# One layer of an S5 / GLA / cross-attention decoder on one core: the S5 factors queued behind the splits of the first projection's weights

## The chip, the core and the metric

The kernel runs on one core of one Trainium2 chip. The metric is the device time of one execution in microseconds (us), the median of the timed runs. The engines are TensorE (PE in the profile, its weight loads PEld), VectorE (DVE), ScalarE (ACT), GpSimd (POOL) and SyncE (SP), which here only issues transfers.

## The reference, cut to what matters

The layer takes 1024 tokens of 1024 numbers. The change touches the beginning of the layer: the input projection and the preparation of the S5 head group.

```
z = h @ w_in                              # h = layer_norm(x); columns u | q k | v | r | gate rank
y_ssm = s5_mixer(z[..., :512], lam, log_step, b, c, d, w_glu, b_glu)
y_gla = gla_mixer(q, k, v, r, g_lr, ...)
...
step = exp(log_step); a = exp(lam * step)            # 32 groups x 64 complex states
f = (a - 1) / lam                                    # f_re, f_im: num * conj(lam) / |lam|^2
bb = f * b                                           # complex, (group, state, 16)
bu = einsum(u, bb); s = associative_scan(a, bu); y = Re(c s) + d u
...
h = LN(alpha h + concat(y_ssm, y_gla) @ w_out); h = LN(alpha h + cross_attention(h, mem)); h = LN(alpha h + mlp(h))
```

## The kernel before, in words

**Products in split float32.** Every large product is made of three products of rounded halves. `split` (L150) makes the halves of a tile: ScalarE writes the rounded high half (`hi`), and then VectorE or GpSimd writes the rest (`lo = src - hi`). `mm3` (L160) issues hi x hi, hi x lo and lo x hi for each 128-wide slice. So a weight tile can be used by the first product of a slice when its `hi` is there, and must have its `lo` by the third. Weights arrive 256 rows at a time (`wcols`, L203): a transfer into a `raw` buffer, of which there are four, and a split into a `w` buffer, of which there are five. Which engine makes the `lo` is chosen by a bit mask; for the u weights the mask `MWU` is 7: pieces 0, 1 and 2 on VectorE, piece 3 on GpSimd.

**The beginning of the layer.** Some work on the memory tokens comes first. Then eight tiles of 128 tokens are normalised and transposed (`embed`), interleaved with the r columns of the projection (`z_block` with `wr`), with `r_epi` behind each. Then come the small gate projection (L529 to L535), the last r block (L536) and the split of the four u weight pieces (`wu`, L537). The last r block and the u weights share buffers: piece 0 of `wu` sits in the fifth buffer and is split early, and pieces 1 to 3 can be split only when the last r block has passed the matching piece of `wr`.

**The S5 factors.** Lines 555 to 716 compute everything that depends only on the S5 parameters, nearly all on VectorE and nearly all on 128 x 16 tiles named `prm` and `par`: exponentials, sine and cosine, the powers `pw`, the rotation tables `E0` and `E1`. Lines 677 to 692 then compute the factor f (`nre`, `den`, `fre`, `fim`). Lines 693 to 698 multiply it with b on GpSimd into `Bb`, and lines 701 to 716 build comparison masks for a later stage.

**Batches of S5.** The 16 pairs of groups go in eight batches of two pairs. A batch passes through the stages `s5_t0` (L749: three outer products on VectorE: C with the powers, `Vt`, 128 x 288 wide; `Bb` with the powers, `wtmp`, 128 x 256 wide; `E0` with `E1`, `rot`, 128 x 256 wide, which runs on GpSimd for all batches but the first, since `CM` is 1), `s5_t1` (transposes), `s5_t2` (taps), `s5_m1` (loads u), `s5_m2` (scan) and `s5_m3` (output). In the traces the tiles of a batch are named `s`; the order rows number them, `s_1341` for the first batch and `s_1360` for the second.

**The u, q, k and v projections.** `z_stream` (L891) yields blocks of 24 products of 128x512. The first two are u columns 0 to 127 for the two halves of the tokens, and so on; behind each of the first four blocks comes a `gate` (L540): one small product, three ScalarE passes, two VectorE operations (`gst`) and a transfer. `Filler.run(n)` runs the stream for n units, where a block yields 5.1. Before the change `fill.run(FP)` with `FP` = 30 runs six blocks, and then the first S5 stages follow.

**What sets the order.** The program is written as one stream. A scheduler places each engine's instructions by its own estimates, as dependences allow, and each engine then executes its list strictly in that order. So the source order around the change is a priority, not the order on the engine. The helper `behind()` (L131) makes the VectorE instructions inside its block queue behind the VectorE instruction traced last.

Of the kernel before, what the change touches and what calls it, by code (L numbers as in the profile page):

```python
# [1 line left out]

# [29 lines left out]
FP = 30  # L32
# [49 lines left out]
def hybrid_layer(  # L82
# [8 lines left out]
    nc = tc.nc  # L91
    V = nc.vector
# [31 lines left out]
    def slot(name, shape, dtype=F32):  # L124
        return arena.tile(shape, dtype, tag="s", name=name)
# [2 lines left out]
        return psp.tile(list(shape), F32, tag=tag, bufs={"d": 3, "s": 3, "g": 2}[tag], name="ps_" + tag)  # L128


    def behind():  # L131

        return tc.issue_after(next(i for i in reversed(nc.cur_bb.bb.instructions) if i.engine == V.engine))

    def ts(e, o, i, s1, s2=None, op0=ALU.mult, op1=None):
        if s2 is None:
# [53 lines left out]
    def eng(bits, i):  # L190
        return V if bits >> i & 1 else G


    def weight(src, shape, e=nc.vector, hl=None):

        raw = rawp.tile(shape, F32, tag="raw", name="raw")
        nc.sync.dma_start(out=raw, in_=src)
        if hl is None:
            hl = wp.tile([P, 2] + list(shape[1:]), F32R, tag="w", name="hl")
        split(hl[:, 0], hl[:, 1], raw, e=e)  # L200
        return hl

    def wcols(src, k0, c0, e=nc.vector, hl=None):  # L203
        return weight(src[k0 * P:(k0 + 2) * P, c0:c0 + 512].rearrange("(k p) n -> p k n", p=P), [P, 2, 512], e, hl)
# [75 lines left out]
    for b in range(4):  # L280
        z = (b + 1) % 3 * 512 + 512
# [47 lines left out]
    def alternate(*streams):  # L329

        streams = [(iter(z), n) for z, n in streams]
        while streams:
            for z in list(streams):
                for _ in range(z[1]):
                    c = next(z[0], None)
                    if c is None:
                        streams.remove(z)
                        break
                    yield c
# [81 lines left out]
    def z_block(w, tok, t, epi):  # L421
        po = bank()
        for k in range(8):
            mm3(po, lambda i: tok(h0(k, i), t), lambda j: w[k // 2][:, j, k % 2, :], k == 0, k == 7)
        epi(t, po)
# [14 lines left out]
    fill = Filler(mem_stream([0], "g", slot("wo0", [P, 2, 2, 2, 512], F32R)))  # L440
# [61 lines left out]
    def pt(n=1):  # L502
        i = scr_n[0]
        scr_n[0] += n
        return scr[:, i, :] if n == 1 else scr[:, i:i + n, :]

    e = V
# [27 lines left out]
        act(glr[th], po[0:32])  # L535
    z_block(wr, tok_block, NT - 1, r_epi)  # L536
    wu = [wcols(w_in, 2 * kp, 0, eng(MWU, kp)) for kp in range(4)]  # L537
    srs.pop()()

    def gate(th, a):  # L540
# [60 lines left out]
    def cmul(e, o_re, o_im, a_re, a_im, b_re, b_im, t):  # L601
        tt(e, o_re, a_re, b_re, ALU.mult)
        tt(e, t, a_im, b_im, ALU.mult)
        tt(e, o_re, o_re, t, ALU.subtract)
        tt(e, o_im, a_re, b_im, ALU.mult)
        tt(e, t, a_im, b_re, ALU.mult)
        tt(e, o_im, o_im, t, ALU.add)
# [56 lines left out]
    for Et, cnt in ((E0, 16), (E1, 8)):  # L664
        G.memset(Et[:, 0, 0, :], 1.0)
        G.memset(Et[:, 1, 0, :], 0.0)
        n = 1
        while n < cnt:
            bc = [z.unsqueeze(1).to_broadcast([P, n, NJ]) for z in (pr, pi_)]
            cmul(e, Et[:, 0, n:2 * n, :], Et[:, 1, n:2 * n, :], Et[:, 0, 0:n, :], Et[:, 1, 0:n, :],  # L670
                 bc[0], bc[1], te[:, 0:n, :])
            o = (pt(), pt())
            cmul(e, o[0], o[1], pr, pi_, pr, pi_, tw[:, 0, :])
            pr, pi_ = o
            n *= 2

    nre, den, fre, fim = (pt() for _ in range(4))
    tt(e, nre, mag1, cs, ALU.mult)
# [189 lines left out]
    def s5(stage_, i):  # L868
        if i < NBT:
            if stage_ is s5_t0:  # L870
                bat[i] = Batch(i)
            stage_(bat[i])

    for i in range(2):
        s5(s5_t0, i)


    qk = slot("qk", [P, 4, SEQ])
# [12 lines left out]
    def z_stream():  # L891

        wqk = []
        for fo in range(4):
            us = stage.tile([P, T, P], F32, tag="kv", bufs=1, name="us")
            for th in range(2):
                po = z_fm(wu, fo, th)
                act(us[:, :, th * 64:(th + 1) * 64], po.rearrange("p (c t) -> p t c", t=T))
                if th:
                    nc.scalar.dma_start(out=u_d[fo * P:(fo + 1) * P], in_=us)  # L900
                if gates:
                    gate(*gates.pop(0))
                if fo == 3:
                    wqk += [wcols(w_in, 2 * kp, 512, eng(MQK, kp)) for kp in (2 * th, 2 * th + 1)]
                yield 5.1

        wv = []
        for fo in range(4):
            for th in range(2):
                po = z_fm(wqk, fo, th)  # L910
                act(qk[:, fo, th * 512:(th + 1) * 512], po, scale=0.125 if fo < 2 else 1.0)
                if fo == 3:
                    wv += [wcols(w_in, 2 * kp, 1024, eng(MVV, kp)) for kp in (2 * th, 2 * th + 1)]
                yield 5.1

        for t in range(NT):
            if t == 1:
                wgl.append(wcols(w_glu, 0, 0))
            po = bank()
            for k in range(8):  # L920
                mm3(po, lambda i: tok_block(h0(k, i), t), lambda j: wv[k // 2][:, j, k % 2, :], k == 0, k == 7)
            vs = stage.tile([P, 512], F32, tag="rt", bufs=3, name="vs")
            act(vs, po)
            nc.scalar.dma_start(out=v_d[t * P:(t + 1) * P, :], in_=vs)
            yield 5.1

    mem_rest = mem_stream([1, 2, 3], "d")
    fill = Filler(z_stream(), mem_rest)
    fill.run(FP)
    s5(s5_m1, 0)  # L930
    s5(s5_t1, 0)
    s5(s5_t2, 0)
# [63 lines left out]
    def y_split(th, k):  # L996
        hi, lo = (ya(0, th)[:, i, k, :].rearrange("p (c t) -> p c t", t=T) for i in range(2))
        with behind():
            split(hi, lo, Y0[:, k, :].rearrange("p (t c) -> p c t", t=T)[:, th * 64:(th + 1) * 64, :], scale=0.25)
# [11 lines left out]
    def glu_stream():  # L1011

        for k in range(4):
            nc.sync.dma_start(out=Y0[:, k, :], in_=y_d[k * P:(k + 1) * P].rearrange("f t c -> f (t c)"))
        for k in range(4):
            if k == 2:
                wgl.append(wcols(w_glu, 2, 0))
            split(glu_s[0][:, k, :], glu_s[1][:, k, :], Y0[:, k, :])
        yield 0
        for fo in range(4):  # L1020
            for th in range(2):
                cs_ = slice(th * 512, (th + 1) * 512)
                po = bank()
                for k in range(4):
                    mm3(po, lambda i: wgl[k // 2][:, i, k % 2, fo * P:(fo + 1) * P], lambda j: glu_s[j][:, k, cs_],
                        k == 0, k == 3)
                sg = sg_[th]
                act(sg, po, AF.Tanh, scale=0.25, bias=bglu[:, fo:fo + 1])
                stt(V, Y0[:, fo, cs_], sg, 1.0, Y0[:, fo, cs_], ALU.add, ALU.mult)
                yield 2.6  # L1030
        for th in range(2):
            for k in range(4):
                y_split(th, k)
                yield 0.5
        load_res(0)

    def out_stream():

        load_res(1)
        w = []  # L1040
        for n in range(2):
            w += [wcols(w_out, 2 * kp, n * 512, eng(MWS, 2 * n + kp)) for kp in range(2)]
        yield 0
        for n in range(2):
            for t in range(NT):
                po = bank()
                for k in range(4):
                    mm3(po, lambda i: ya.lhs(k, i, t), lambda j: w[2 * n + k // 2][:, j, k % 2, :], k == 0, k == 3)
                r = res(t)[:, n * 512:(n + 1) * 512]
                stt(V, r, r, ALPHA, po, ALU.mult, ALU.add)  # L1050
                yield 2.6

    fill = Filler(alternate((glu_stream(), 1), (fill, 1)), out_stream())
# [342 lines left out]
    for _ in range(2):  # L1396
        z = wp.tile([P, 2, 2, 512], F32R, tag="w", name="w1q")
# [202 lines left out]
    def half_stats(m):  # L1600
        with behind():
            for n in range(2):
                stats(m, n)
            if m == 3:
                first.extend(last_stats(range(4)))

    def norm_half():
        with behind():
            last_norm(*first.pop(0))
# [127 lines left out]
```

## Time and profile before

| | us |
|---|---|
| median of 3 runs | 1384.01 (1383.97 to 1388.86) |
| the profiled execution, its own time | 1385.14 |
| its span | 1383.3 |
| what lies around the span | 1.8 |
| PE busy in the span | 1336.5 (97%) |
| DVE busy | 966.8 (70%) |
| ACT busy | 569.6 (41%) |
| POOL busy | 410.4 (30%) |

A row of the timeline gives the start, the time, the engine, the line, the operation, out<-in, shapes and count; behind it in brackets the idle time before it and what ended it. Consecutive operations on one engine overlap a little, so that the sum of their times is more than the time from the first start to the last end. A line such as L142 or L163 is a helper's: the tile names tell which step it is. A row of waits has the total, the number of times and the longest, in us.

### The profile page before, as it was taken

To read this page: it belongs to the slowest core of one execution; us is meant where nothing else is said; L and a number is where in the kernel's file an instruction comes from. 1 tells how busy PE (TensorE), PEld (TensorE's weight loads), DVE (VectorE), ACT (ScalarE), POOL (GpSimd) and SP (SyncE) were. 2 spreads that over 40 slices of the span, in tenths; PEclk is the share of its full clock that TensorE was granted. 3 is DMA by queue.
4 is the path that set the end of the run, shared out by engine and by line. 5 is a ranking of instruction groups with operands and counts; after the bars stand their busy time and mean duration, and the time that the engine had idled before them with its cause. 6 is when DMAs were issued, how large, how long until landed. Compare 5 with 4: busy or idle time off the path is not lost. (4 is left out here: it accounts for less than half of the span.)

```text
span 1383.3 us, 18805 instructions
## 1 busy us (share of the span) xinstructions
PE 1336.5 (97%) x6824; PEld 1110.4 (80%) x6824; DVE 966.8 (70%) x1713; ACT 569.6 (41%) x950; POOL 410.4 (30%) x315
## 2 busy tenths in 40 slices
PE   6798999999999999999999999999999999999997
PEld 6575777788899888788888778788888888888886
DVE  8999587947965369844468866665565576668785
ACT  4432532323545244433123755455456343344441
POOL 1663133502334133000013124433332242003353
PEclk9999999999999999999999999999999999999999
DMA  9832332454576130310212657654446984235432
GB/s 303 264 122 69 120 104 65 126 171 137 201 258 214 48 92 23 122 31 0 62 46 61 183 167 228 214 167 158 160 139 238 328 309 145 94 110 163 136 107 91
DMA packets 155512, 199.81 MB, mean 144 GB/s; under 512 B 16294, under 2 KB 86044, under 8 KB 155292
## 3 DMA queue, kind: packets, MB, share of 16 engines
q1 hardware_dynamic: 143536, 179.44, 40.0%
q10 hardware_dynamic: 11884, 19.17, 3.7%
q8 instruction: 54, 0.88, 0.3%
q14 instruction: 38, 0.31, 0.1%
HBM read 140.38 MB, written 58.20 MB: 144 GB/s over the span
## 5 line engine op out<-in xcount | busy, mean ns | idle before, releaser
L163 PE MATMUL ps_d<-xt,w1q 128*128 128x512 f32 x576 | 137.2, 389 | 0.0
L163 PEld LDWEIGHTS ps_d<-xt,w1q 128*128 128x128 f32 x576 | 108.1, 188 | 22.4
L163 PE MATMUL ps_s<-cell 128*128 128x512 f32 x432 | 113.0, 389 | 0.0
L163 PE MATMUL ps_d<-cell 128*128 128x512 f32 x432 | 106.0, 389 | 0.4 <-DVE hid L142 0.4
L163 PE MATMUL ps_d<-h0T,hl 128*128 128x512 f32 x384 | 93.1, 400 | 5.8 <-DVE hl L142 5.8
L163 PEld LDWEIGHTS ps_d<-cell 128*128 128x128 f32 x432 | 81.0, 188 | 17.6 <-DVE hid L142 0.8
L163 PEld LDWEIGHTS ps_s<-cell 128*128 128x128 f32 x432 | 81.1, 188 | 16.8
L163 PE MATMUL ps_d<-hl,h0T 128*128 128x512 f32 x384 | 92.5, 398 | 1.3 <-DVE h0T L142 1.3
L148 ACT ACTIVATE hl<-raw 128x1024 fp32r<-128x1024 f32 x62 | 65.3, 1064 | 68.9 <-PE ps_d L163 61.9
L163 PEld LDWEIGHTS ps_d<-h0T,hl 128*128 128x128 f32 x384 | 72.8, 192 | 25.7 <-DVE hl L142 6.2
L163 PE MATMUL ps_d<-hl,y 128*128 128x512 f32 x384 | 92.4, 395 | 0.0
L163 PE MATMUL ps_g<-xb,w1q 128*128 128x512 f32 x384 | 92.1, 391 | 0.0
L163 PE MATMUL ps_d<-hl,p 128*128 128x512 f32 x384 | 89.0, 391 | 0.0
L148 ACT ACTIVATE hid<-hid 128x512 f32<-128x512 f32 x112 | 70.8, 632 | 38.9 <-DVE hid L142 37.1
L163 PEld LDWEIGHTS ps_d<-hl,h0T 128*128 128x128 f32 x384 | 72.2, 191 | 17.4 <-DVE h0T L142 1.8
L142 DVE TENSOR_TENSOR cell<-ha,cell 128x1024 fp32r<-128x1024 f32 x56 | 82.4, 1472 | 3.3 <-ACT cell L148 3.3
L163 PEld LDWEIGHTS ps_d<-hl,p 128*128 128x128 f32 x384 | 71.6, 188 | 14.6
L163 PEld LDWEIGHTS ps_g<-xb,w1q 128*128 128x128 f32 x384 | 71.5, 188 | 14.6
L163 PEld LDWEIGHTS ps_d<-hl,y 128*128 128x128 f32 x384 | 70.7, 188 | 14.6 <-issue 0.3
L142 DVE TENSOR_TENSOR hl<-raw,hl 128x1024 fp32r<-128x1024 f32 x50 | 66.4, 1336 | 21.0 <-ACT hl L148 20.5
L148 ACT ACTIVATE w1q<-raw 128x512 fp32r<-128x512 f32 x80 | 50.1, 629 | 69.3 <-PE ps_d L163 27.3
L142 POOL TENSOR_TENSOR hl<-raw,hl 128x1024 fp32r<-128x1024 f32 x12 | 33.6, 2806 | 142.0 <-ACT hl L148 142.0
(296 smaller groups left out, 2802.8 us busy)
## 6 DMA issues: line engine op xcount, KB each, us to landing
g_d<-hid SPq DMA_DIRECT2D x112, 256.0 KB
ha<-g_d SPq DMA_DIRECT2D x56, 512.0 KB
raw<-in_w_ff_dram SPq DMA_DIRECT2D x40, 512.0 KB
b<-in_w_ff_dram SPq DMA_DIRECT2D x32, 512.0 KB
raw<-in_w_mkv_dram SPq DMA_DIRECT2D x16, 512.0 KB
raw<-in_w_in_dram SPq DMA_DIRECT2D x16, 512.0 KB
wq<-in_w_mq_dram SPq DMA_DIRECT2D x8, 512.0 KB
xs<-in_x_dram SPq DMA_DIRECT2D x8, 512.0 KB
```

The lines of the kernel that those rows point to most:

```text
L142: e.tensor_tensor(out=o, in0=a, in1=b, op=op)
L148: A.activation(out=o, in_=i, func=f, **kw)
L163: PE.matmul(o, lhs(i), rhs(j), start=first and n == 0, stop=last and n == 2, skip_group_check=more)
```

## The change

Three edits. First, `behind` takes the instructions to queue behind as arguments. Second, the VectorE instruction traced last after the u weights are split is kept as `split_u` (it is the `lo` of piece 2), and every VectorE instruction written from the computation of `nre` (L677 before) up to the end of the first batch's `s5_t0` queues behind it. Third, the second batch's `s5_t0` is no longer written next to the first's, but after two blocks of the u projection. Instructions of GpSimd and of ScalarE are not pinned; they follow through their dependences and the scheduler's order.

```diff
-    def behind():
-        return tc.issue_after(next(i for i in reversed(nc.cur_bb.bb.instructions) if i.engine == V.engine))
+    def traced(e):
+        return next(i for i in reversed(nc.cur_bb.bb.instructions) if i.engine == e.engine)
+
+    @contextmanager
+    def behind(*ins):
+        with ExitStack() as z:
+            for i in ins or (traced(V),):
+                z.enter_context(tc.issue_after(i))
+            yield
...
     wu = [wcols(w_in, 2 * kp, 0, eng(MWU, kp)) for kp in range(4)]
+    split_u = traced(V)
...
+    order = ExitStack()
+    order.enter_context(behind(split_u))
+
     nre, den, fre, fim = (pt() for _ in range(4))
...
-    for i in range(2):
-        s5(s5_t0, i)
+    s5(s5_t0, 0)
+    order.close()
...
-    fill.run(FP)
+    fill.run(10)
+    s5(s5_t0, 1)
+    fill.run(FP - 10)
```

On VectorE, around the splits of pieces 1 and 2 of `wu` (`hl<-raw,hl`), the order before the change reads as follows; `prm` and `par` are S5 parameter tiles, `s_1360` is the second batch.

```order
L142 TENSOR_TENSOR s_1360<-par 128x256
L142 TENSOR_TENSOR prm<-par,prm 128x16
L142 TENSOR_TENSOR par<-par,prm 128x16
L142 TENSOR_TENSOR prm<-prm 128x16
L142 TENSOR_TENSOR hl<-raw,hl 128x1024
L142 TENSOR_TENSOR par<-par,prm 128x16
L142 TENSOR_TENSOR prm<-prm 128x16 x2
L142 TENSOR_TENSOR hl<-raw,hl 128x1024
```

After the change (line 142 is line 150 there) the same place, and the beginning of what is pinned; `s_1341` is the first batch.

```order
L150 TENSOR_TENSOR par<-par,prm 128x64
L150 TENSOR_TENSOR prm<-prm 128x16 x2
L150 TENSOR_TENSOR hl<-raw,hl 128x1024 x2
L150 TENSOR_TENSOR prm<-prm 128x16 x4
L150 TENSOR_TENSOR prm<-par,prm 128x16
L150 TENSOR_TENSOR prm<-prm 128x16
L150 TENSOR_TENSOR prm<-par,prm 128x16
L150 TENSOR_TENSOR s_1341<-par 128x288
L695 RECIPROCAL prm<-prm 128x16
```

The two splits now stand next to each other, ahead of every operation on a batch, and behind all of the powers and rotation tables, of which 31 small operations stood behind the first split before.

On GpSimd, before the change, from the end of the six operations of `Bb` (`prm<-prm` and `par<-par,prm` are the last two of them) past the r block's epilogue (`rt`) and the split of piece 3 to the second batch's rotation:

```order
L142 TENSOR_TENSOR prm<-prm 128x256
L831 MEMSET s_1360 128x2
L142 TENSOR_TENSOR par<-par,prm 128x256
L142 TENSOR_TENSOR rt<-rt,prm 128x512
L790 MEMSET s_1341 80x2x128
L879 MEMSET qk 128x1
L1065 MEMSET S 128x256
L142 TENSOR_TENSOR hl<-raw,hl 128x1024
L142 TENSOR_TENSOR s_1360<-par 128x256 x4
L142 TENSOR_TENSOR s_1360<-s_1360 128x256 x2
```

After the change, where the second batch has the name `s_1436`:

```order
L150 TENSOR_TENSOR rt<-rt,prm 128x512
L1079 MEMSET S 128x256
L150 TENSOR_TENSOR hl<-raw,hl 128x1024
L891 MEMSET qk 128x1
L150 TENSOR_TENSOR s_1436<-par 128x256 x4
L150 TENSOR_TENSOR s_1436<-s_1436 128x256 x2
L843 MEMSET s_1436 128x2
L150 TENSOR_TENSOR par<-prm 128x256
L717 IOTA prm 128x128
L150 TENSOR_TENSOR prm<-prm 128x256
```

The six operations of `Bb` have moved from ahead of the split of piece 3 to behind the second batch's rotation, which itself still follows that split.

On VectorE, at the first of the four gates (`gst`), before the change:

```order
L142 TENSOR_TENSOR s_1341<-s_1341 128x256
L137 TENSOR_SCALAR prm<-prm 128x128
L142 TENSOR_TENSOR s_1360<-s_1360 128x256
L145 SCALAR_TENSOR_TENSOR mask<-prm 128x64
L142 TENSOR_TENSOR s_1360<-s_1360 128x256
L137 TENSOR_SCALAR prm<-prm 128x128
L139 TENSOR_SCALAR gst<-ps_s,bgate 128x512
L145 SCALAR_TENSOR_TENSOR mask<-prm 128x64
L142 TENSOR_TENSOR hl<-raw,hl 128x1024
```

After the change:

```order
L145 TENSOR_SCALAR prm<-prm 128x128
L150 TENSOR_TENSOR s_1341<-par 128x256
L153 SCALAR_TENSOR_TENSOR mask<-prm 128x64
L150 TENSOR_TENSOR s_1341<-s_1341 128x256 x2
L147 TENSOR_SCALAR gst<-ps_s,bgate 128x512
L150 TENSOR_TENSOR s_1436<-par 128x288
L150 TENSOR_TENSOR gst<-gst 128x512
L150 TENSOR_TENSOR s_1436<-par 128x288 x3
```

The first gate now stands behind the whole first batch and behind the last mask; the second batch's twelve VectorE operations stand between the first gate's first operation and the second gate's last, where before they were all ahead of the first gate's.

The order on PE is the same in both programs. On ACT one small copy of the second batch moves behind the u weights' high halves. On SP one later weight load moves behind the u loads of the first two batches.

More of the change, by code (lines that the diff above doesn't have):

```diff
@@ L1 @@
-from contextlib import ExitStack
+from contextlib import ExitStack, contextmanager
 import concourse.bass as bass
```

## The prediction

> **What bounds the kernel now.** The page comes first: PE is busy for 97% of the span, so only what makes PE wait, or makes its clock fall, can change the time.
>
> ```profile
> span 1383.3 us, 18805 instructions
> PE 1336.5 (97%) x6824; PEld 1110.4 (80%) x6824; DVE 966.8 (70%) x1713; ACT 569.6 (41%) x950; POOL 410.4 (30%) x315
> ```
>
> The waits of PE in the first 420 us come next. The longest single one is a wait for `hl`, a `lo` of the u weights, which is where the change acts.
>
> ```profile
> PE ps_d L163 <- DVE hl L142: 5.8, 1, 5.8
> ```
>
> The timeline of PE shows where it is and what follows it.
>
> ```profile
> 117.32 1.98 PE L163 MATMUL ps_d<-h0T,hl 128*128 128x512 f32 x8
> 125.08 6.15 PE L163 MATMUL ps_d<-h0T,hl 128*128 128x512 f32 x16 [5.78 <-DVE hl L142]
> 131.15 1.12 PE L543 MATMUL ps_s<-prm 32*128 32x512 f32 x2
> ...
> 138.94 5.73 PE L163 MATMUL ps_d<-h0T,hl 128*128 128x512 f32 x24
> ...
> 151.32 1.12 PE L543 MATMUL ps_s<-prm 32*128 32x512 f32 x2
> ```
>
> Eight products of the first u block run: six on piece 0 and two on piece 1. Then PE stands for 5.78 us until the `lo` of piece 1 exists. The remaining 16 products take 6.15 us, though a block of 24 takes 5.73, which is 0.239 each and 3.82 for 16. The windows of one microsecond say why.
>
> ```profile
> 122.00:123.00 1.00, 0.00 (x0) 1.00 0.00 0
> 123.00:124.00 1.00, 0.00 (x0) 0.52 0.00 0
> 129.00:130.00 1.00, 1.00 (x4) 0.57 0.84 250
> 130.00:131.00 1.00, 1.00 (x6) 1.00 1.03 305
> ```
>
> The granted clock (the column before the last two) falls to half some 4 us into the wait, and is full again only at 130.
>
> Why the split comes late is read from VectorE's timeline and its groups between 95.1 and 123.8 us.
>
> ```profile
> 95.19 0.43 DVE L569 COPY par<-prm 128x512 f32<-128x512 f32 x1 [0.33 <-POOL xs L142]
> ...
> 118.24 2.37 DVE L142 TENSOR_TENSOR prm<-prm 128x16 f32<-128x16 f32 x1
> ...
> 123.81 1.22 DVE L142 TENSOR_TENSOR hl<-raw,hl 128x1024 fp32r<-128x1024 f32 x1
> ```
>
> ```profile
> L142 DVE TENSOR_TENSOR s<-par 128x288 f32<-128x288 f32 x8 | 4.1, 518 | 0.0
> L142 DVE TENSOR_TENSOR s<-par 128x256 f32<-128x256 f32 x6 | 2.5, 419 | 0.0
> ...
> L145 DVE SCALAR_TENSOR_TENSOR rt<-rt,ps_d 128x512 f32<-128x512 f32 x2 | 1.4, 680 | 0.0
> ...
> L142 DVE TENSOR_TENSOR par<-par,prm 128x16 f32<-128x16 f32 x8 | 1.3, 165 | 0.0
> ...
> L142 DVE TENSOR_TENSOR s<-s 128x288 f32<-128x288 f32 x2 | 0.9, 449 | 0.0
> L145 DVE SCALAR_TENSOR_TENSOR s<-s 128x288 f32<-128x288 f32 x2 | 0.9, 448 | 0.0
> L142 DVE TENSOR_TENSOR s<-s 128x256 f32<-128x256 f32 x2 | 0.8, 422 | 0.0
> ```
>
> VectorE has no idle time from 95.19 to 123.81: it works through factors and batches, and the split stands in that list. Its input was there long before, since ScalarE wrote the three high halves from 114.76 on:
>
> ```profile
> 114.76 2.94 ACT L148 ACTIVATE hl<-raw 128x1024 fp32r<-128x1024 f32 x3
> ```
>
> **The change part by part.**
>
> *The splits go ahead of the batches.* Out of the list before the split go 20 batch operations, 4.1 + 2.5 + 0.9 + 0.9 + 0.8 = 9.2 us busy. An operation starts about 0.08 before its forerunner ends, so this is 7.6 us of clock. Into it come 31 small operations on powers and tables that stood behind the first split: at 0.165 each 5.1 us at most, 2.6 with the overlap. The operation at 118.24, 16 elements wide, took 2.37 us. GpSimd's timeline shows why, and what GpSimd does next.
>
> ```profile
> 117.78 2.80 POOL L142 TENSOR_TENSOR hl<-raw,hl 128x1024 fp32r<-128x1024 f32 x1 [3.87 <-ACT hl L148]
> 130.47 4.41 POOL L142 TENSOR_TENSOR s<-par 128x256 f32<-128x256 f32 x4 [9.89 <-DVE prm L142]
> 134.84 1.73 POOL L142 TENSOR_TENSOR s<-s 128x256 f32<-128x256 f32 x2
> ```
>
> It ended at 120.61, when GpSimd's split of piece 3 ended at 120.58. In the new order VectorE should be at the splits before that begins, which takes off another 2.3 us. So VectorE comes to them at 123.81 - 7.6 - 2.3 + 2.6 = 116.5 (latest, without the last two savings, 123.81 - 7.6 + 5.1 = 121.3). I take 116.5, since the operations of `Bb`, which ran beside this stretch, have left it too. The `lo` of piece 1 is then ready at 117.7 and that of piece 2 at 118.9. PE needs them at 117.32 + 1.98 = 119.30 and, six products on, at 120.7. Piece 3, on GpSimd, ends at 120.6 and is needed 20 products in, at 122.1; its place behind ScalarE is not later than before. So the wait goes whole: **-5.78**. With it goes the clock's fall, 6.15 - 3.82: **-2.33**. Late next would be piece 3, with 1.5 us to spare.
>
> From then on PE is 8.1 us ahead: the first gate's product at 123.05 instead of 131.15, the fourth's at 143.2 instead of 151.32.
>
> *What the pinned work delays.* Behind the splits stand some 14 small operations and a reciprocal, the last r block's epilogue, three integer and ten mask operations, and the first batch's 18. The integer and mask operations are priced by this group of the stretch from 124.9 to 143 us:
>
> ```profile
> L137 DVE TENSOR_SCALAR prm<-prm 128x128 f32<-128x128 f32 x5 | 1.1, 221 | 0.1
> ```
>
> The clock of all, with nothing in the way, each row's mean less the overlap of 0.08: 15 x 0.09 + 2 x 0.6 + 13 x 0.14 + 6 x 0.37 + 12 x 0.34, so 10.7 us, which I round up to 11.4 for the integer types, and an end at 118.9 + 11.4 = 130.3. In the way is GpSimd, which now runs the second batch's rotation (4.41 + 1.73 = 6.1 us) directly behind piece 3 and then `Bb`, six operations of the same 256 columns, so 6.1 at most. If VectorE loses all of that it ends at 142.5. Then comes the first gate's `gst`.
>
> ```profile
> 138.58 0.74 DVE L139 TENSOR_SCALAR gst<-ps_s,bgate 128x512 f32<-128x512 f32 x1
> ...
> 140.65 0.68 DVE L142 TENSOR_TENSOR gst<-gst 128x512 f32<-128x512 f32 x1
> ```
>
> It ran at 138.58 and I take 139.5 for it, near the upper end, because `Bb` needs the pinned `fre` and `fim` and the batch needs `Bb`. Who waits for it: the fourth gate's product, as there are three banks of `ps_s`, at 143.2; and ScalarE at the third gate, whose buffer comes free with the first gate's transfer. Until 143.2 it costs PE nothing; at the upper end of 142.5 still nothing, though the third gate then starts late on ScalarE. The gates had cover, which the waits between 120 and 200 us show:
>
> ```profile
> DVE gst L142 <- ACT gst L148: 3.6, 2, 3.1
> ...
> DVE gst L139 <- ACT gst L148: 2.1, 1, 2.1
> ```
>
> VectorE waited 5.7 us for ScalarE within the gates. The second batch's twelve operations, 6 x 0.37 + 6 x 0.34 = 4.3 us, now fill this time instead of preceding it. PE comes to the first batch's transposes here:
>
> ```profile
> 163.39 0.60 PE L783 MATMUL ps_g<-ident,s 128*128 128x128 f32 x4
> ```
>
> That is 155.3 in the new time, over 12 us after the first batch is done, and the second batch's are 4.4 us later, for operations that end near 147. I take **+0.3** for the additions to the taps, which stand behind the last gate in VectorE's list; bounds 0 and +5, if the chain of gates on ScalarE runs late. The order of SP moves one weight load behind u loads; its piece belongs to q and k, behind eight blocks of u, so it costs nothing. The factor's own operations leave the stretch before 95 us, where they are some eight of 0.09: nothing, bounds -1 and +0.5.
>
> Sum: -5.78 - 2.33 + 0.3 = **-7.8**. Against the profiled execution, 1385.14 - 7.8 = 1377.3. That execution lies 1.1 above the median, so on the median's scale 1384.01 - 7.8 = **1376.2**. After 200 us PE's list is the same and PE sets the pace, so the lead should be carried to the end.
>
> **A shorter wait that stays, weighed against the skill.** An earlier wait of PE shows what a rest of 2 to 3 us would cost.
>
> ```profile
> 77.86 0.65 PE L251 MATMUL ps_s<-ident,xs 128*128 128x128 f32 x4 [2.36 <-POOL xs L142]
> 78.27 7.35 PE L163 MATMUL ps_d<-hl,h0T 128*128 128x512 f32 x24
> ```
>
> After only 2.36 us of idleness 24 products took 7.35 instead of 5.73, so 1.6 us more. The Trainium skill ("TensorE: Matmul & The Clock Gate", Part 1) says that the clock is halved after at least one idle window of about 3.4 us; by that a rest under 3.4 us would cost no clock. The row disagrees, and I price by the row.
>
> **The rivals.**
>
> *Part of the wait stays.* If VectorE reaches the splits at 121.3, the `lo` of piece 1 comes at 122.5, PE waits 3.2 us and the clock takes 1.6 more: 7.8 - 4.8, so a gain of 3.0 and 1381.0. For it: small operations stretch next to GpSimd, as at 118.24. Against it: from 117.7, where I put the end of the first split, to 119.3 there are 1.6 us of margin. Chance 0.13.
>
> *The gates come late.* If the first `gst` comes at 145 or its successors each push ScalarE back, PE loses 2 to 5 us at the fourth gate or at the transposes: a gain of about 4, 1380. Chance 0.12.
>
> *The lead is given back.* A later wait, on a transfer or on VectorE in the S5 loop, might absorb it: 1384. PE's later waits are short, which speaks against it. Chance 0.07.
>
> *Slower.* The pinned block, GpSimd's rotation, `Bb` and the first batch become one chain: `Bb` waits for the rotation and for `fim`, the batch waits for `Bb`, the first gate for the batch. The place is VectorE's first `gst`. Each microsecond past 143.2 is one on PE's fourth gate; at 151.3 the lead is gone, and at 158 the time is 1391. For that, the 48 pinned operations would need 39 us, 0.8 us each, three and a half times the 11.4 of their sum. The Trainium skill ("SBUF — State Buffer", Who interferes with whom) says that a VectorE operation with two SBUF inputs and a GpSimd operation that reads SBUF lock each other out for a whole instruction. By that rule alone, which the operation at 118.24 bears out, VectorE loses at most GpSimd's busy time, which is the 142.5 above. Chance 0.08.
>
> **How the numbers follow.** The forecast has 0.60. About 0.5%, or 6.9 us, is what a measurement of this kernel can tell from no change, and it lies at 1377.1, only 0.9 from the forecast. The spread of the forecast is -1.5 to +1.5 (the bounds of the small terms), so I count 0.50 of the 0.60 beyond it and 0.10 short of it. Faster 0.50; same 0.10 + 0.13 + 0.12 + 0.07 = 0.42; slower 0.08. The range runs from 1374.2, two below the forecast, to 1382.5, which takes in the first two rivals.
>
> **What would show it.** Right: no PE wait for `hl` near 119, the clock at 1.00 from 117 to 131, the first gate's product near 123.05, the fourth's near 143.2 without a wait, the first transposes near 155.5. Wrong: a rest of the wait at 119; `gst` on VectorE later than 143 with PE idle before the fourth gate; or a lead of 8 us at 155 that is smaller at 350 or 600.

## The result, and the profile after

| | before | after |
|---|---|---|
| median, us | 1384.17 (8 runs, 1381.14 to 1388.86) | 1376.62 (8 runs, 1373.27 to 1381.32) |
| ratio after/before, 95% interval | | 0.9949 (0.9938 to 0.996) |
| profiled execution, its own time, us | 1385.14 | 1376.45 |
| its span, us | 1383.3 | 1374.4 |

The change takes 7.55 us off the median; the ratio puts the gain at 0.51%, with an interval from 0.4% to 0.62%. The forecast was 1376.2. The page of the changed kernel first:

```profile
span 1374.4 us, 18808 instructions
PE 1333.9 (97%) x6824; PEld 1108.2 (81%) x6824; DVE 968.6 (70%) x1713; ACT 569.6 (41%) x950; POOL 410.6 (30%) x315
```

The busy times are almost those of before; PE's is 2.6 us shorter, of the size of what the half clock behind the old wait had cost (the clock fell at other places too, not at the same ones in both traces). The rest that went is waiting. Of PE's wait for a `lo` of the u weights, this is left among its waits of the first 420 us (total, times, longest):

```profile
PE ps_d L171 <- DVE hl L150: 0.6, 1, 0.6
```

PE's timeline shows the u block at 117.69, with one short stop after 14 products instead of a long one after eight, and then the first gate, the fourth, and the first batch's transposes:

```profile
117.69 3.33 PE L171 MATMUL ps_d<-h0T,hl 128*128 128x512 f32 x14
121.64 2.56 PE L171 MATMUL ps_d<-h0T,hl 128*128 128x512 f32 x10 [0.61 <-DVE hl L150]
124.13 1.12 PE L552 MATMUL ps_s<-prm 32*128 32x512 f32 x2
...
144.27 1.12 PE L552 MATMUL ps_s<-prm 32*128 32x512 f32 x2
145.32 11.18 PE L171 MATMUL ps_d<-h0T,hl 128*128 128x512 f32 x48
156.34 0.60 PE L795 MATMUL ps_g<-ident,s 128*128 128x128 f32 x4
```

Against the rows of before these three are earlier by 131.15 - 124.13 = 7.02, 151.32 - 144.27 = 7.05 and 163.39 - 156.34 = 7.05. In this execution the block itself started 0.37 later (117.69 against 117.32), so the block gained 7.4. None of that was lost from the first gate to the transposes: there is no bracket at the fourth gate. The time by which PE is ahead of the first trace of before, at the same product, is called the lead from here on. The granted clock (the column before the last two), which fell to half in the old wait, stays at full speed around the stop:

```profile
121.00:122.00 1.00, 0.39 (x3) 1.00 0.36 137
122.00:123.00 1.00, 1.00 (x6) 1.00 0.41 23
```

Why a stop is left is seen on VectorE and GpSimd. VectorE's timeline first, with the two splits of pieces 1 and 2 in one row, what follows them, and the first gate:

```profile
117.02 4.56 DVE L150 TENSOR_TENSOR hl<-raw,hl 128x1024 fp32r<-128x1024 f32 x2
121.51 1.60 DVE L150 TENSOR_TENSOR prm<-prm 128x16 f32<-128x16 f32 x4
...
138.47 0.73 DVE L147 TENSOR_SCALAR gst<-ps_s,bgate 128x512 f32<-128x512 f32 x1
139.13 0.43 DVE L150 TENSOR_TENSOR s<-par 128x288 f32<-128x288 f32 x1
139.50 0.67 DVE L150 TENSOR_TENSOR gst<-gst 128x512 f32<-128x512 f32 x1
```

GpSimd's timeline over the same time, piece 3's split and then the second batch's rotation:

```profile
117.67 2.83 POOL L150 TENSOR_TENSOR hl<-raw,hl 128x1024 fp32r<-128x1024 f32 x1 [4.90 <-ACT hl L156]
...
120.51 4.00 POOL L150 TENSOR_TENSOR s<-par 128x256 f32<-128x256 f32 x4
```

The second split's own row shows how the 4.56 us are divided:

```profile
118.16 3.43 DVE L150 TENSOR_TENSOR hl<-raw,hl 128x1024 fp32r<-128x1024 f32 x1
```

The first split took 1.2 us, the second 3.4. It ends at 121.58, 1.08 after GpSimd's split ended at 120.50: the second split moved only when GpSimd was done (e8 below tests this), and PE stood for it from 121.03 to 121.64.

The gates had their cover, the time by which their delayed work may be late without PE waiting for it. VectorE waits for ScalarE within them hardly any more (5.7 us before), and ScalarE's third gate starts late, held by the transfer of the first, with no PE wait behind it:

```profile
DVE gst L150 <- ACT gst L156: 0.2, 1, 0.2
```

```profile
142.71 0.69 ACT L156 ACTIVATE gst<-ps_s,bgate 128x512 f32<-128x512 f32 x1 [4.45 <-DMA gk_d<-gst]
```

The spans of the two profiled executions differ by 8.9 us, 1.8 more than the 7.05 at the transposes. What came on top lies behind 200 us and is not the change's. The trace of before has a wait in the S5 loop that the trace of after lacks, with the clock's fall behind it:

```profile
217.15 0.49 PE L852 MATMUL ps_s<-s 64*128 64x128 f32 x4 [1.60 <-DVE s L142]
```

```profile
219.00:220.00 1.00, 1.00 (x12) 0.50 0.00 0
```

Between 215 and 225 us the lead grows from 7.09 to 9.94, and 1.1 of that is lost again behind 1000 us. e1 and e3 below, which still have the old wait for the split, gain 2.8 and 2.5 in the same place against the first trace of before; so this part was a loss of that one execution. e5 and e6 show too that such waits come and go between executions of one kernel.

### The profile page after: what moved, and what is told of

It is laid out like the page before. It is cut to its first block, busy times and chain, and to the rows that moved or that the text cites. A ratio compares the mean times of both kernels' runs of the same rounds, so it can differ in the third digit from the quotient of the medians.

```text
span 1374.4 us, 18808 instructions
## 1 busy us (share of the span) xinstructions
PE 1333.9 (97%) x6824; PEld 1108.2 (81%) x6824; DVE 968.6 (70%) x1713; ACT 569.6 (41%) x950; POOL 410.6 (30%) x315
```

## The experiments

The theory that the runs were to test: the pin (VectorE's queueing behind `split_u`) brings the splits forward, PE's wait and the half clock behind it vanish, and cover up to 143 us hides what is delayed. The rivals: the place of the second batch does it; the wait alone counts and the clock does not; the gates eat the lead; the lead is lost again in the S5 loop. All ratios below are set against runs of the kernel before on the same chip, so they are not the quotients of the medians in the table. "Block to gate" is the time from the first product of the u block to the first gate's product, which does not depend on when an execution reaches the block.

| | edit | median, us | ratio to before | block to gate, us |
|---|---|---|---|---|
| before | | 1384.17 | 1 | 13.83 |
| after | | 1376.62 | 0.9949 (0.9938 to 0.996) | 6.44 |
| e1 | no pin | 1384.96 | 0.9991 (0.998 to 1.0002) | 13.22 |
| e2 | pin, both batches in it | 1379.57 | 0.9953 (0.9936 to 0.997) | 6.60 |
| e3 | before, the wait filled | 1382.33 | 0.9977 (0.9962 to 0.9992) | 11.70 |
| e4 | after, a batch twice | 1379.00 | 0.9948 (0.9934 to 0.9963) | 6.61 |
| e5 | before again, one run | 1383.76 | | 14.40 |
| e6 | after again | 1376.63 | 0.9948 (0.993 to 0.9966) | 6.58 |
| e7 | piece 3 on VectorE too | 1378.24 | 0.9957 (0.994 to 0.9973) | 6.78 |
| e8 | pin from `E1` on | 1376.00 | 0.9937 (0.9915 to 0.9959) | 5.53 |
| e9 | only the factors pinned | 1388.29 | 1.0025 (1.0009 to 1.0041) | 12.73 |
| e10 | as e8 | 1373.35 | 0.9911 (0.9889 to 0.9932) | 5.53 |
| e11 | after, beside e12 | 1376.30 | 0.9949 (0.9933 to 0.9965) | 6.20 |
| e12 | as e8 | 1375.79 | 0.9946 (0.993 to 0.9961) | 5.53 |

**e1: the later place of the second batch alone.**

```diff
-    order.enter_context(behind(split_u))
```

> The kernel after without the pin: the second batch's t0 is written two blocks later, but nothing queues behind the splits. Theory (the pin does it): the second batch's operations still stand ahead of the splits in VectorE's list, so PE waits about 5.8 us at 119 with the clock at half until 130, and the time is that of before within 0.15% (ratio 0.9985 to 1.0015). Rival (the later place of the second batch does it): the splits come about 3 us earlier, the wait shrinks to 2 or 3 us, ratio 0.996 to 0.997.

PE's timeline has the old wait:

```profile
126.09 5.50 PE L171 MATMUL ps_d<-h0T,hl 128*128 128x512 f32 x16 [5.81 <-DVE hl L150]
```

The time is that of before. Without the pin the batches' operations stand ahead of the splits again (VectorE reached the first one at 124.83), wherever the second batch is written. So the later place alone brings nothing. Block to gate is 0.6 us shorter than in before although the wait is the same: the 16 products behind it took 5.50 us instead of 6.15, and in e5, behind the same wait, 6.74. The half clock lasts 6.8 us in all three traces, but begins 2.4, 3.7 and 5.0 us into the wait (e1, before, e5), so a different share of it falls on products.

**e2: the pin alone, both batches inside it.**

```diff
-    s5(s5_t0, 0)
+    for i in range(2):
+        s5(s5_t0, i)
...
-    fill.run(10)
-    s5(s5_t0, 1)
-    fill.run(FP - 10)
+    fill.run(FP)
```

> The kernel after with the second batch's t0 left next to the first's, inside the pin. Theory: the wait for the splits goes as in the kernel after; the first gate's VectorE operation comes at about 143 instead of 138.5, still ahead of the fourth gate's product at 144.3, and ScalarE's chain of gates runs some 4 us later, which costs 0.5 to 1.5 us at the first batch's transposes: ratio to before 0.9955. Rival (without the later place the gates eat the lead): a PE wait of 3 us or more before the fourth gate or the transposes, ratio 0.998 or more.

The wait is gone here too (0.76 left). The first gate is later on VectorE, ScalarE's third gate waits longer, and PE stands once behind the transposes:

```profile
142.46 0.76 DVE L147 TENSOR_SCALAR gst<-ps_s,bgate 128x512 f32<-128x512 f32 x1
```

```profile
146.77 0.69 ACT L156 ACTIVATE gst<-ps_s,bgate 128x512 f32<-128x512 f32 x1 [8.71 <-DVE gst L150]
```

```profile
158.68 1.04 PE L809 MATMUL ps_g<-s,par 64*16 64x128 f32 x8 [0.96 <-ACT s L156]
```

The pin alone gives nearly everything. The gates eat about 1 us of it: at 142.46 the first `gst` is at the end of its cover, and only the chain on ScalarE shows through.

**e3: the kernel before, with the wait filled.** 24 products whose result nobody reads stand in front of the third slice of the first u block.

```diff
+            if fo == 0 and th == 0 and k == 2 and w is wu:
+                idle = bank("g")
+                for n in range(24):
+                    PE.matmul(idle, h0(n % 8, 0)[:, 0:P], h0(n % 8, 1)[:, 0:512], start=True, stop=True)
```

> The kernel before with 24 added products of 128x512 in an unused bank in the place where PE waits for the split of piece 1; their result is read by nobody. The wait for the split stays, but PE is busy through it (24 x 0.239 = 5.7 us). Theory (2.3 us of the gain are the clock): granted clock 1.00 from 117 to 131, the 16 products after the wait take 3.8 us instead of 6.15, the first gate's product comes 2.2 us earlier than in before, ratio 0.9984. Rival (the clock costs nothing, only the wait counts): the first gate's product comes where it was, ratio 1.000.

PE's timeline, with the added products at 118.60, and one of the windows:

```profile
118.60 5.60 PE L887 MATMUL ps_g<-h0T,h0T 128*128 128x512 f32 x24
...
125.02 3.99 PE L163 MATMUL ps_d<-h0T,hl 128*128 128x512 f32 x16 [0.36 <-DVE hl L142]
128.94 1.12 PE L543 MATMUL ps_s<-prm 32*128 32x512 f32 x2
```

```profile
123.00:124.00 1.00, 1.00 (x6) 1.00 0.00 0
```

The split comes no earlier; what is different is the clock, at 1.00 where it was 0.52. The 16 products behind it took 3.99 instead of 6.15, and the first gate came 13.83 - 11.70 = 2.1 us sooner. So the clock's share of the forecast (2.33) is real, and work that computes nothing buys it; the ratio's interval, 1.1 to 5.3 us below before, agrees. Its size differs from execution to execution: against the 3.99 at full clock, the 16 products lost 1.5 us in e1, 2.2 in before and 2.8 in e5.

**e4: the end of the cover.** The first batch's `s5_t0` runs twice inside the pin, so that the first gate's `gst` is pushed back.

```diff
     s5(s5_t0, 0)
+    s5_t0(bat[0])
```

> The kernel after with the first batch's t0 done twice (the second time writes the same values), all behind the pin: 18 more VectorE operations of 0.35 us ahead of the first gate, so 6 to 8 us. Theory (the gates have 5.8 us of cover, 138.5 against 144.3): the first gate's VectorE operation comes at 145 to 147, PE waits 1 to 3 us at the fourth gate and 2 to 4 more at the transposes, because ScalarE's gates run 7 us late: time 3 to 6 us above the kernel after, ratio to before 0.998. Rival (the gates are hidden anyway): no PE wait of over 1 us there, ratio 0.995 as in the kernel after.

`gst` ran at 144.95. PE now does wait before the fourth gate, and the clock falls behind that wait:

```profile
145.75 1.12 PE L552 MATMUL ps_s<-prm 32*128 32x512 f32 x2 [1.82 <-DVE gst L147]
146.80 12.79 PE L171 MATMUL ps_d<-h0T,hl 128*128 128x512 f32 x48
```

```profile
147.00:148.00 1.00, 1.00 (x5) 0.89 0.45 174
148.00:149.00 1.00, 1.00 (x4) 0.50 0.23 88
```

The cost on the spot is 1.82 of wait and 12.79 - 11.18 = 1.61 of clock, 3.4 us, and its place, the fourth gate's product, is the one that the prediction gave. The further 2 to 4 us that were expected at the transposes did not come. The lead falls from 7.44 to 3.97 there and is still 3.97 at 215 us. Yet the ratio is that of after. In the profiled execution 1.5 us were made up because the clock did not fall at about 320, as it did in after's trace. For the medians, of four runs only, it stays open what paid for the cost; it is shown at its place, but not in the total.

**e5 and e6: both kernels once more.**

> The kernel before once more, for its trace alone. In the first trace of before PE lost about 2.9 us at 217 (a wait of 1.6 for VectorE in the S5 loop and the clock behind it), which the kernel after did not lose. Theory (what differs behind 200 us is chance from execution to execution): the wait at the S5 outputs differs in place or size from the first trace, the 5.8 us wait for the splits is the same within 0.3. Rival (it belongs to before's order): the same wait of 1.6 us at the same instruction.

> The kernel after once more, as the measure for the next two on one chip. Theory: 0.6 us of wait for the second split at 121, because it stands behind GpSimd's split of piece 3; first gate's product 7.0 us ahead of before; ratio 0.995.

The wait for the split is there in e5 (5.8) and 0.75 long in e6. In the S5 loop it is the other way round than in the first two traces, where before waited 1.6 us and after 0.3. The waits there, e5 (before) and then e6 (after):

```profile
PE ps_s L852 <- DVE s L142: 1.0, 1, 1.0
```

```profile
PE ps_s L864 <- DVE s L150: 2.3, 2, 2.0
```

One of them stands at the same product in both orders and differs in size only: 1.60 (before), 1.03 (e5), 0.58 (e3), 0.27 (after), 0.28 (e6), 1.22 (e2). The other one of e6, 2.0 us long, is also in e1, which has the old wait for the split. So neither belongs to one of the two orders.

In e6 PE reached the u block 1.87 us later than in the first trace of before, was 5.4 ahead of that trace behind it, so 7.3 in the block, and ended 5.5 ahead. Over the traces of after, e6, e7, e8 and e10 the lead at the end differs from that at 215 us by 0 to 5.3 us, in both directions (the first trace of before, against which the lead is counted, itself lost 2.9 us at 217). Every single total carries this, so only medians of several runs are compared.

**e7: all three late splits on VectorE.**

```diff
-MWU = 7
+MWU = 15
```

> The kernel after with piece 3 of the u weights split on VectorE too (mask 15). GpSimd then begins the second batch's rotation some 5 us earlier, at about 113, beside the small table operations that VectorE has left before the splits. Theory (VectorE and GpSimd lock each other out operation by operation): each of those some 40 operations takes about 0.6 us instead of 0.1 while the rotation runs, VectorE reaches the splits at 120 to 122, PE waits 3 to 5 us for piece 1; ratio to before 0.998. Rival (the wait of 0.6 came only from piece 3's place on GpSimd): no wait for a split, first gate's product 0.6 us earlier than in the kernel after.

Neither came true. VectorE and GpSimd, one timeline each:

```profile
118.31 4.60 DVE L150 TENSOR_TENSOR hl<-raw,hl 128x1024 fp32r<-128x1024 f32 x3
```

```profile
115.99 4.16 POOL L150 TENSOR_TENSOR s<-par 128x256 f32<-128x256 f32 x4 [3.55 <-issue]
```

GpSimd, rid of the split, began the second batch's rotation 4.5 us earlier (120.51 in after). VectorE reached the splits 1.3 us later, at 118.31 and not at 120 to 122, then took three in the time that two had taken. PE waited 0.27 us, its 16 products ran at VectorE's pace (4.60 instead of 3.82), and block to gate is 0.3 us longer than in after. The wait changed its place, not its size.

**e8, e10 and e12: the splits ahead of GpSimd's.** The pin opens at the second rotation table, so that VectorE stands idle when the high halves come.

```diff
+    order = ExitStack()
     for Et, cnt in ...
+        if Et is E1:
+            order.enter_context(behind(split_u))
...
-    order = ExitStack()
-    order.enter_context(behind(split_u))
```

> The kernel after with the pin begun earlier, at the smaller rotation table (E1): some 30 small operations more queue behind the splits. Theory: VectorE reaches the splits at about 113, so both are done before GpSimd begins piece 3 at 117.7; no PE wait for a split, first gate's product 0.6 us earlier than in the kernel after; the first gate's VectorE operation comes 2 to 4 us later, at 141 to 142, which may cost up to 1 us at the transposes; time within 1 us of the kernel after. Rival (the second split is late for another reason than GpSimd): the wait of 0.6 stays.

> The kernel of e8 a second time, for the interval: the pin is open from the second table on, so that the second split ends before GpSimd's third piece begins. Theory: no wait of TensorE for a split, first gate 0.5 to 1 us earlier than in the changed kernel relative to the block's start, and a ratio to the kernel before of 0.993 to 0.996, 0 to 2 us below the changed kernel's 1376.6. Rival (the 0.9 us is lost again in the S5 loop by waits that differ from execution to execution): ratio 0.995 or above, not different from the changed kernel.

> The changed kernel itself, on the same chip as e12, so that the two are compared through the same runs of the kernel before. Both theories: ratio 0.9935 to 0.9965, a rest of TensorE's wait for a split of 0.5 to 0.8 us.

> The kernel of e8 and e10 beside the changed kernel. Theory (what it removes is the 0.6 us of wait and 0.3 us of slower products behind it, nothing else): 0.5 to 1.5 us below e11, ratio 0.0005 to 0.001 lower. Rival (the earlier splits also change what follows, as the ratio 0.9911 of e10 suggests): 3 to 4 us below e11, intervals that do not overlap.

VectorE, GpSimd and PE in e8:

```profile
113.91 2.59 DVE L150 TENSOR_TENSOR hl<-raw,hl 128x1024 fp32r<-128x1024 f32 x2 [1.47 <-ACT hl L156]
```

```profile
116.68 2.42 POOL L150 TENSOR_TENSOR hl<-raw,hl 128x1024 fp32r<-128x1024 f32 x1 [4.91 <-ACT hl L156]
```

```profile
116.70 5.60 PE L171 MATMUL ps_d<-h0T,hl 128*128 128x512 f32 x24
122.23 1.12 PE L552 MATMUL ps_s<-prm 32*128 32x512 f32 x2
```

Both splits took 2.59 us instead of 4.56, ended before GpSimd's began, and PE ran all 24 products without a stop: block to gate 5.53 in all three traces, 0.7 to 1.1 less than in those of after. So what held the second split was GpSimd's operation. The first `gst` came at 139.58, 1.1 us later than in after, and the lead does not change between the first gate and the transposes (8.92 and 8.95). In the totals the gain is small: e12 stands 0.5 us below e11, as the theory said, with intervals that overlap nearly wholly. e10's 1373.35 was the lowest median of all; e8 and e12 don't repeat it. At 215 us the leads of e10 and e12 are equal (8.53 and 8.46), so what sets their traces apart comes later. This is the lowest time that the runs found, 0.5 to 0.9% below before. Its 0.7 to 1.1 us over after are shown in the block, and not in the total.

**e9: the factors pinned, the batch not.**

```diff
-    s5(s5_t0, 0)
     order.close()
+    s5(s5_t0, 0)
```

> The pin now covers only the five factors and the masks; the first batch's 12 operations are listed without it, right after it, and the second batch two blocks later as in the changed kernel. Theory (what the pin moves on VectorE's path are the first batch's 12 operations and GpSimd's rotation, which in the order of this kernel stand ahead of the splits again): TensorE's wait for a split stays, between 3 and 6 us, the first gate's product starts at 129 to 131.5 in the profile's time, and the time is 1380 to 1385, ratio 0.998 to 1.001. Rival (the factors and masks alone are what delays the splits; the batch finds room beside them): wait below 1 us, first gate near 124, ratio near 0.995.

PE's timeline shows three stops in the block:

```profile
121.15 1.65 PE L171 MATMUL ps_d<-h0T,hl 128*128 128x512 f32 x6 [1.69 <-DVE hl L150]
123.09 1.66 PE L171 MATMUL ps_d<-h0T,hl 128*128 128x512 f32 x6 [0.29 <-DVE hl L150]
128.22 2.08 PE L171 MATMUL ps_d<-h0T,hl 128*128 128x512 f32 x4 [3.47 <-POOL hl L150]
130.22 2.07 PE L552 MATMUL ps_s<-prm 32*128 32x512 f32 x2
132.23 7.99 PE L171 MATMUL ps_d<-h0T,hl 128*128 128x512 f32 x24
```

GpSimd's timeline shows the longest one's cause, the second batch's rotation ahead of piece 3:

```profile
119.15 2.58 POOL L150 TENSOR_TENSOR s<-par 128x256 f32<-128x256 f32 x2 [6.59 <-DVE prm L150]
...
125.81 2.36 POOL L150 TENSOR_TENSOR hl<-raw,hl 128x1024 fp32r<-128x1024 f32 x1
```

On VectorE, 12 operations of 128x288, the first product (`Vt`) of both batches, stand ahead of the splits again, which begin at 119.88 and 121.82; the expectation's 12 operations of the first batch are not these, as that batch has 18. The waits sum to 5.45 us, within the 3 to 6 of the theory, and the clock's fall now reaches into the next block (7.99 instead of 5.76). From the block's start to the end of that next block PE needs 2.1 us more than before (12.73 - 13.83, with 2.2 more for the products and 1.0 for the gate), and the time is above that of before, 3 us past the 1385 that was the end of the expected range. So it matters that the batch is pinned: the pin on VectorE also decides, through the scheduler, what stands ahead on GpSimd, which no line of the source says.

## Why the prediction was right, point by point

**The wait (-5.78): right in its cause, too large by the stop that is left.** VectorE came to the splits at 117.02, or 116.65 with the block's later start taken off; the forecast was 116.5. The first `lo` was in time: PE ran over it without a stop. The second was not. The step that failed: "The `lo` of piece 1 is then ready at 117.7 and that of piece 2 at 118.9." Piece 2's came at 121.58. The sentence ahead of it had put VectorE at the splits before GpSimd's split begins, which held for the first of the two only. The working set GpSimd's split at 117.8 to 120.6 and the second split at 117.7 to 118.9, on top of one another, and had itself read at 118.24 what happens to an operation in that place: 16 elements took 2.37 us. That price was taken off as a saving and not charged to whatever would come to stand there. The runs show the price: 4.56 us for two splits beside GpSimd's, 2.59 (e8) ahead of it. The Trainium skill ("SBUF — State Buffer", Who interferes with whom) says that a VectorE instruction with two SBUF inputs contends with a GpSimd instruction that reads SBUF, and that the issue order decides who blocks. The traces agree with it.

**The clock (-2.33): right, with a size that is one execution's.** It stayed at 1.00, and e3 took 2.1 us off by the clock alone. Behind the same wait it cost 1.5 us in e1 and 2.8 in e5, so the 2.33 of the first trace lay in the middle by luck. The price of 1.6 us for a short wait, which the rival of a wait that stays was given from the row at 77.86, is one execution's too: in e3, whose program is that of before there, the same wait of 2.34 us cost no clock (the last section).

**What the stop cost.** Both terms together were -8.1; the block gained 13.83 - 6.44 = 7.4. Without any stop it gains 13.83 - 5.53 = 8.3 (e8). The 0.9 between the two is the stop, 0.61 in the row and some 0.3 that no row shows (the last section).

**The delayed work: right.** The first `gst` was forecast for 139.5 and ran at 138.47, the fourth gate for 143.2 and ran at 144.27, without a wait. The second batch's operations fell into VectorE's waits within the gates (5.7 us before, 0.2 after). e2 (142.46: no wait at the fourth gate) and e4 (144.95: 3.4 us lost) bear out the point of 143.2 from which it would have cost there. But at 142.46, in e2, PE lost about 1 us through ScalarE's chain, where the prediction had set nothing for 142.5. The +0.3 for the taps' additions did not show: the lead is 7.05 at the fourth gate and at the transposes.

**The lead to the end: right, within the variation.** It is still 7.09 at 215 us, and the medians differ by 7.55, against a sum of -7.8. That they meet within 0.3 us is partly luck: a stop of 0.9 was not counted, the +0.3 did not show, and the clock's term is 0.6 smaller in e1 and 0.6 larger in e5. The rival in which the lead is given back later fell: the waits at L864 (0.3 us in the first trace of after, 2.3 in e6) differ from execution to execution, as those of before do (1.6 and 1.0). One later wait, for `hid` behind 1000 us, is longer in after's trace (1.2 us against 0.4), but it is 1.3 in e1, without the pin, and 0.4 in e11, which is after again.

**The rivals.** Part of the wait did stay, but 0.6 of it and not 3.2, and because of GpSimd's split and not because VectorE came late. The late gates and the slow chain did not come; e4 shows that they were one batch's work away. The bound of 0.5% was put at 0.9 us from the forecast; the measured ratio lies on it.

## What to carry to other kernels

A wait ahead of the busiest engine is worth its length and, where the clock falls, the slower products behind it (1.5 to 2.8 us for one and the same wait here), and an order on one engine that lets the awaited operation go first can collect both, if the work it delays has cover: work out the time at which that cover ends, as with the 143.2 here. When an operation with two SBUF inputs is moved on VectorE, look at what GpSimd runs at the new time, and charge the whole of that operation to whoever comes second. A pin on one engine also moves the lists of the others, as e9 and e7 show on GpSimd, so read those lists before and after. And price what a short wait costs in clock from several executions, as one and the same wait near 77 us cost 1.6 us in one and nothing in another.

## What the runs showed of the hardware that was not expected

**A short stop of PE costs 0.3 us more than its row.** Without a stop, block to gate is 5.53. The excess, and the wait's row, in five executions: 0.91 and 0.61 (after), 1.07 and 0.76 (e2), 1.08 and 0.78 (e4), 1.05 and 0.75 (e6), 0.67 and 0.37 (e11). The difference is 0.30 or 0.31 each time, at full clock in the windows of after. The rows show where it comes from: consecutive products overlap, so 24 of them take 5.60 us in one row, and 14 and 10 with a stop between them 3.33 and 2.56, together 5.89.

**The clock changes on a beat of its own, so a short wait costs clock in one execution and not in the next.** In e3, the program of before in this place, a wait of 2.34 us had no fall behind it, where before's 2.36 us had one (24 products in 7.35):

```profile
77.78 0.65 PE L251 MATMUL ps_s<-ident,xs 128*128 128x128 f32 x4 [2.34 <-POOL xs L142]
78.20 5.73 PE L163 MATMUL ps_d<-hl,h0T 128*128 128x512 f32 x24
```

The time of a fall is read from the windows, here two of before:

```profile
78.00:79.00 1.00, 1.00 (x7) 0.83 0.00 0
```

```profile
218.00:219.00 1.00, 1.00 (x11) 0.80 0.23 68
```

A mean of 0.83 in a window that begins at 1.00 and ends at 0.50 puts the fall a third before its end. So the clock of before fell at 78.66, 123.03 and 218.61. These times lie 13 and 28 times 3.413 us apart, and so it is in all 14 traces: the falls of one trace are whole multiples of 3.41 us apart, and each lasts 3.41 us or two or three times that (the last one is cut off by the end of the program). Thirteen traces have the wait of 2.33 to 2.36 us near 77. Counting stretches of 3.41 us on from the falls of the same trace gives the beat there. In the seven traces in which the wait lay nearly whole within one stretch (2.1 us or more of it), the clock fell at the end of the stretch; in the six in which the beat cut the wait into parts of at most 1.83 us, it did not fall. A fall can therefore come when PE is long at work again, as in e4 (it stood from 143.93 to 145.75, and the clock fell at 147.78). No single length decides: 1.38 us of idleness within the stretch were enough in e4, 1.60 in before at 217, and 1.61 in e6 at 246 were not. What else counts is open. The stops of 0.6 to 0.8 us within the block did not slow the products behind them (10 in 2.56 or 2.57). The Trainium skill ("TensorE: Matmul & The Clock Gate", Part 1) names an idle window of about 3.4 us as what halves the clock. Idle times well below that did so here, in some executions.

**GpSimd pays as well.** Its split of piece 3 took 2.83 us in after, where VectorE's first split still ran for 0.57 us when it began, 2.59 in e11, where 0.31 were left, and 2.42 (e8) and 2.36 (e9) where no split of VectorE's was running. In after, e2, e4, e6 and e11 it ends 2.26 or 2.27 us after VectorE's first split does, and VectorE's second split ends 1.08 us after it: each one moves when the other engine's operation is over.
